# Norm roots by Newton steps on DVE, and transposes between the halves of the output projection, in a two-layer decoder trunk

## The chip, the cores and the metric

The kernel runs on one core of one Trainium2 chip. The core has a matrix engine (PE, with its weight loads PEld), a vector engine (DVE), an activation engine (ACT), a general engine (POOL) and a queue engine (SP) that here only issues DMAs. Each engine takes its instructions strictly in order. The metric is the device time of one execution in microseconds (us).

## What is computed

Two layers on 512 tokens of width 1024. Every sublayer is x += PostNorm(f(PreNorm(x))), and each norm needs one reciprocal root per token:

```python
def rms_norm(x, g):
    y = x * lax.rsqrt(jnp.mean(x * x, axis=-1, keepdims=True) + RMS_EPS)
    return y * g

def reference(...):
    for layer in range(DEPTH):                       # DEPTH = 2
        h = rms_norm(x, mix_pre_g[layer])
        if layer < N_A:                              # layer 0
            m = pool_mixer(h, pool_w[layer], pool_scale[layer])
        else:                                        # layer 1
            ... # k, v from rms_norm(x, kv_norm_g), rope, shared
            m = swa_sink_attention(q, kk, vv, sinks[j]) @ w_o[j]
        x = x + rms_norm(m, mix_post_g[layer])
        f = conv_glu_ffn(rms_norm(x, ffn_pre_g[layer]), ffn_w_in[layer], ffn_conv_w[layer],
                         ffn_conv_b[layer], ffn_w_out[layer])
        x = x + rms_norm(f, ffn_post_g[layer])
    return x
```

conv_glu_ffn is an up-projection to 2 x 2816 channels, a causal convolution of width 3, GeGLU, and a down-projection.

## The kernel before, in words

The 512 tokens are four row blocks of 128 (b = 0 to 3), one token to a partition, so a norm's root is one value per partition: a tile of 128x1. A factor of a product is split into a high and a low part (`wh`/`wl` for weights, `xTh`/`xTl` for activations, `gh`/`gl` for the FFN's hidden values), and a product is three matmuls (`mm3`, lines 306 to 308). The high part is a copy on ACT, the low part a subtraction on DVE, or on POOL in `low` (line 398, through line 193).

**Order.** Line 1147 opens `tc.manual_schedule(engines=ORDERED)`, and ORDERED (line 1131) names PE, ACT, DVE and POOL: on these four the program's order is the order of execution, and only the semaphores between them are added.

**A root.** `rstd_of` (line 243) squares both halves of a row on ACT, each with its sum into a column of `ss` (line 247). After the first half POOL adds epsilon (`add_eps`, 254); after the second, `rstd_end` adds the two sums (257) and raises them to -0.5 (258), both on POOL. There are 32 roots: four blocks times mix_norm, post_norm and pre_norm in layer 0, the FFN's post norm in both layers (`root` in pass2), `pre_a` before the attention, and post_norm and pre_norm after it.

**The stages that hold roots.** I call them A to D.

- A, the mixer of layer 0 (lines 402 to 441). `mix_norm` scales x; `mix_pool` and `mix_map` are matmuls; `post_norm` (264) multiplies by the gain straight from PSUM (272) and adds to x (274); `pre_norm` (286) makes the next input (291); `transpose_in` (294) turns it on PE (299) and splits it (302 on ACT, 303 on DVE). `low` splits the first two units of FFN weights in between, eight quarters in all, on ACT (189) and POOL (193). `start0` then runs the up-projection `up` of the units j = 0 and 1 for blocks 0 and 1, with the transposes of blocks 2 and 3 in between.
- B, the end of the down-projection of layer 0, `pass2` (612). Two block products, X[2] and X[3], are summed over p = 0 to 10. Blocks 2 and 3 are ready early: after p = 0 their sums are added (652), squared (671), rooted, multiplied by the gain (676) and added to x (685). `soon(k)` splits the weights (226, 227) and hidden values (636, 637) that later p need: soon(6) those of p = 6 and 7, soon(7) of 8 and 9, soon(8) of 10. `pre_a` and `pre_b` (278, 282) norm x for the attention, and `to_attention` (770) transposes it. The last three p run for blocks 0 and 2 first (i = 0), then for 1 and 3; blocks 0 and 1 are finished after that, while PE runs the k and v projections (`kp`, `vp`) of blocks 2 and 3.
- C, the output projection after the attention (1043 to 1054) and `start1` (1056): per block `o_proj`, `post_norm`, `low`, `pre_norm`, `low`, with the transposes of blocks 0 and 1 in the turns of blocks 2 and 3; then `up` as in A.
- D, the same as B in layer 1, without attention behind it: the end of the kernel.

SP loads weights through two buffers `raw`; a new load is issued when the split of an older unit is done.

Of the kernel before, what the change touches and what calls it, by code (L numbers as in the profile page):

```python
# [8 lines left out]
F32 = mybir.dt.float32  # L9
F32R = mybir.dt.float32r  # L10
I32 = mybir.dt.int32
AF = mybir.ActivationFunctionType
ALU = mybir.AluOpType
PSUM = bass.MemoryType.PSUM

P = 128
S = 512
D = 1024
# [8 lines left out]
EPS = 1e-6  # L27
# [43 lines left out]
def build(nc, tc, ctx, a, out):  # L71
# [3 lines left out]
    pc = ctx.enter_context(tc.tile_pool(name="pc", bufs=1))  # L75
# [18 lines left out]
    xT = new_xT("f0")  # L94
# [19 lines left out]
        o = ch * 4 + k  # L114
        return convs[l][:, o : o + 1]

    mhalf = pc.tile([P, 1], F32, tag="mhalf", name="mhalf")
    nc.gpsimd.memset(mhalf, -0.5)


    raws, slots, homes = {}, {}, {}
# [118 lines left out]
        return t  # L240


    def rstd_of(src, junk, name):

        ss = pc.tile([P, 4], F32, tag="ss", name=f"ss_{name}", bufs=6)
        for h in range(2):
            nc.scalar.activation(junk[h], src[h], AF.Square, scale=1.0 / math.sqrt(D),
                                 accum_out=ss[:, h : h + 1])
            if h == 0:
                add_eps(ss, 0)  # L250
        return rstd_end(ss)

    def add_eps(ss, h):
        nc.gpsimd.tensor_scalar(ss[:, h : h + 1], ss[:, h : h + 1], EPS, None, ALU.add)  # L254

    def rstd_end(ss):
        nc.gpsimd.tensor_tensor(ss[:, 2:3], ss[:, 0:1], ss[:, 1:2], ALU.add)
        nc.gpsimd.tensor_tensor(ss[:, 3:4], ss[:, 2:3], mhalf, ALU.pow)
        return ss[:, 3:4]

    def halves(t):
        return [t[:, h * 512 : (h + 1) * 512] for h in range(2)]
# [72 lines left out]
    xns, xnf = {}, {}  # L335
# [276 lines left out]
    def pass2(l, p2, G2, X, post_row):  # L612


        Z12 = pc.tile([P, D], F32, tag="bc", name=f"Z12_{l}", bufs=2)
        Z11 = pc.tile([P, D], F32, tag="t4", name=f"Z11_{l}", bufs=3)
        Z2 = pc.tile([P, 4 * D], F32, tag="xTh", name=f"Z2_{l}")
        gx = pc.tile([P, 4 * D], F32R, tag="xTl", name=f"gx_{l}")
        Z = {"11": halves(Z11), "12": halves(Z12), "21": halves(Z2[:, 0:D]), "22": halves(Z2[:, D : 2 * D])}
        gains = halves(post_row)  # L620
        G = {}

        def split2(n, m):
            k = min(4 if n == 2 else 2, NP - (4 if n == 2 else 2) * m)
            if n == 2 and m < 2:

                h, lo = (gx[:, (2 * m + c) * 1024 : (2 * m + c + 1) * 1024] for c in range(2))
            else:
                h, lo = (p2.tile([P, 1024], F32R, tag="g", name=f"{c}{n}_{l}_{m}", bufs=8) for c in ("gh", "gl"))
            if n == 2:  # L630
                g = G2[:, 4 * m : 4 * m + k, 2, :]
                o = [t[:, : k * 256].rearrange("p (k t) -> p k t", t=256) for t in (h, lo)]
            else:
                g = G2[:, 2 * m : 2 * m + k, 0:2, :].rearrange("p k q t -> p k (q t)")
                o = [t[:, : k * 512].rearrange("p (k t) -> p k t", t=512) for t in (h, lo)]
            nc.scalar.copy(o[0], g)
            nc.vector.tensor_tensor(o[1], g, o[0].bitcast(F32), ALU.subtract)  # L637
            G[n, m] = (h, lo)

        homes[U_D2[l] + 1] = homes[U_D3[l] + 2] = homes[U_D3[l] + 5] = (p2, "x")  # L640
        for t in ("whx", "wlx"):
            p2.tile([P, 2048], F32R, tag=t, name=f"first_{t}{l}")
        todo = [(2, 0), (2, 1), (2, 2), *((3, m) for m in range(6))]

        def soon(k):
            if k < len(todo):
                n, m = todo[k]
                split((U_D2 if n == 2 else U_D3)[l] + m)
                split2(n, m)

        def add(z, i, q):
            nc.vector.tensor_tensor(Z[z][i], Z[z][i], X[q][i], ALU.add)

        soon(0)
        for i in range(2):
            nc.scalar.copy(Z["11"][i], X[1][i])
            nc.vector.tensor_tensor(Z["21"][i], Z["11"][i], X[6][i], ALU.add)
        soon(1)
        for i in range(2):
            nc.vector.tensor_tensor(Z["12"][i], Z["21"][i], X[5][i], ALU.add)  # L660
        for q in (4, 2, 3):
            X[q] = [bank(f"dn{l}_{q}_{i}") for i in range(2)]
        ss, rs = {}, {}

        def square(z, i, q):

            b, h = i + (2 if z[0] == "2" else 0), int(z[1]) - 1
            first = b not in ss
            if first:
                ss[b] = pc.tile([P, 4], F32, tag="ss", name=f"ss_p_f{l}{b}", bufs=6)  # L670
            nc.scalar.activation(X[q][i], Z[z][i], AF.Square, scale=1.0 / math.sqrt(D), accum_out=ss[b][:, h : h + 1])  # L671
            if first:
                add_eps(ss[b], h)

        def gain(z, i):
            nc.vector.tensor_tensor(Z[z][i], Z[z][i], gains[int(z[1]) - 1], ALU.mult)

        def root(b):
            rs[b] = rstd_end(ss[b])

        def update(b):
            r = rs[b]
            for h in range(2):
                xs = halves(x[b])[h]
                nc.vector.scalar_tensor_tensor(xs, Z[f"{b // 2 + 1}{h + 1}"][b % 2], r, xs, ALU.mult, ALU.add)
                if l == 1:
                    nc.sync.dma_start(out[b][:, h * 512 : (h + 1) * 512], xs)

        def then(f, b):
            if l == 0:  # L690
                f(b)


        for m in range(3):
            for p in range(4 * m, min(4 * m + 4, NP)):
                product(U_D2[l] + m, (p % 4) * 512, G[2, m], (p % 4) * 256, X[4], (0, 1), p == 0, p == NP - 1)
            soon(m + 2)
            if m < 2:
                nc.vector.tensor_tensor(Z["22"][m], Z["12"][m], X[7][m], ALU.add)
                add("21", m, 7)  # L700
                square("22", m, 7)
            else:
                for i in range(2):
                    gain("22", i)
        of = {3: (512, 256), 2: (0, 0)}

        def make(q, p, is_):
            w, go = of[q]
            o = p % 2
            product(U_D3[l] + p // 2, o * 1024 + w, G[3, p // 2], o * 512 + go, X[q], is_, p == 0, p == NP - 1)  # L710

        NT = 3
        for p in range(NP - NT):
            for q in of:
                make(q, p, (0, 1))
            if p == 0:
                for i in range(2):
                    add("21", i, 4)
                    square("21", i, 4)
                    root(2 + i)  # L720
                soon(5)
                for i in range(2):
                    gain("21", i)
                for i in range(2):
                    update(2 + i)
                soon(6)
            if p == 1:
                then(pre_a, 2)
                then(pre_a, 3)
                soon(7)  # L730
                then(pre_b, 2)
                then(pre_b, 3)
            if p == 5:
                then(to_attention, 2)
                soon(8)
                then(split, U_K)
            if p == 6:
                then(to_attention, 3)

        for i in range(2):  # L740
            for q in of:
                for p in range(NP - NT, NP):
                    make(q, p, (i,))
        then(split, U_V)
        add("12", 0, 3)
        square("12", 0, 3)
        add("11", 0, 2)
        square("11", 0, 2)
        root(0)
        gain("12", 0)  # L750
        gain("11", 0)
        add("12", 1, 3)
        square("12", 1, 3)
        update(0)
        then(pre_a, 0)
        add("11", 1, 2)
        square("11", 1, 2)
        root(1)
        gain("12", 1)
        gain("11", 1)  # L760
        then(pre_b, 0)
        update(1)
        then(pre_a, 1)
        then(pre_b, 1)

# [14 lines left out]
    with tc.tile_pool(name="att", bufs=1, reuse_waits="tile") as pa:  # L780
# [4 lines left out]
        nsink = pa.tile([P, NH], F32, tag="nsink", name="nsink")  # L785
        nc.gpsimd.tensor_scalar(nsink, sink, -1.0, None, ALU.mult)
        tab = pa.tile([P, 1], F32, tag="tab", name="tab")
# [146 lines left out]
        to_attention(1)  # L934
        k_T(3, kst[3])
        split(U_Q)
        nc.scalar.activation(tab, mhalf, AF.Exp)
        kst[0] = k_block(0)
        v_block(0)
        split(U_Q + 1)  # L940
# [4 lines left out]
        acc, xnf = {}, {}  # L945
# [33 lines left out]
        os = {}  # L979
# [62 lines left out]
        xT = new_xT("f1")  # L1042
# [2 lines left out]
        u0, u1 = U_IN[1], U_IN[1] + 1  # L1045
        for b in range(NB):
            u = (u0, u1)[b // 2]
            o_proj(1, b, os[1, b])
            post_norm(b, acc[b], post_row, "m1", pa)
            low(u, b % 2 * 2)  # L1050
            if b > 1:
                transpose_in(b - 2, xnf[b - 2], xT, "f1")
            xnf[b] = pre_norm(b, pre_row, "f1")
            low(u, b % 2 * 2 + 1)

# [94 lines left out]
```

## Time and profile before

| what | value |
|---|---|
| median of 3 runs | 946.09 us (945.75 to 950.86) |
| profiled execution | 945.61 us, of which the span from first to last instruction is 943.5 us |
| busy time over the span | PE 911.8, PEld 781.1, DVE 654.3, ACT 469.5, POOL 337.9 us |
| mean granted TensorE clock | 0.988 of full speed |
| instructions on DVE, POOL | 940, 389 |

The profile is of one execution. Starts are in us from the span's first instruction. A line of a timeline is: start, duration, engine, line of the kernel, operation, output tile <- input tiles, shapes, count, and in brackets the idle time of that engine just before it and what ended it. A line of a group has, after the bar, the total busy time, the mean duration of one in ns, and the idle time before them. Where a timeline merges several instructions (x2, x4), the duration runs from the first start to the last end.

### The profile page before, as it was taken

The page shows a single profiled execution, that of the slowest core. Times are in us where ns is not written, and L with a number is a line of the kernel's source. Part 1 is how long each engine was busy: PE and PEld are TensorE (multiplying, and loading weights), DVE is VectorE, ACT ScalarE, POOL GpSimd, SP SyncE. Part 2 cuts the span into 40 slices and gives each one's busy share as a digit, 9 for nine tenths or more (in the row PEclk, how much of TensorE's full clock was granted, in tenths as well). Part 3 has the DMA queues.
Part 4 walks back from the last instruction along what each step waited for, and adds up shares of the span by engine and source line. Part 5 has one row for each costly group of instructions (what it writes and reads, how often), then busy time and mean ns, then how long its engine had stood idle before and what let it go on. Part 6 is the DMA issues. An engine that isn't in the chain of part 4 may idle for free.

```text
span 943.5 us, 12767 instructions
## 1 busy us (share of the span) xinstructions
PE 911.8 (97%) x4702; PEld 781.1 (83%) x4702; DVE 654.3 (69%) x940; ACT 469.5 (50%) x823; POOL 337.9 (36%) x389
## 2 busy tenths in 40 slices
PE   9999999999999999899999996999999999999996
PEld 8888888888888877799899885988888888888784
DVE  5878888765567788545999747466555565677886
ACT  5645444533345566454788634433333433455562
POOL 3725444433341002325566226144444433410001
PEclk9999999999999999899999997999999999999998
DMA  8356899855555664740112214444555555456652
GB/s 304 123 192 222 324 332 319 296 198 189 190 177 149 217 211 147 278 162 19 45 46 91 90 45 149 142 179 179 187 206 198 197 204 191 160 164 196 222 186 87
DMA packets 43024, 170.10 MB, mean 180 GB/s; under 512 B 5073, under 2 KB 6609, under 8 KB 34898
## 3 DMA queue, kind: packets, MB, share of 16 engines
q1 hardware_dynamic: 41810, 160.90, 48.7%
q10 hardware_dynamic: 1152, 8.39, 2.3%
q8 instruction: 37, 0.61, 0.3%
q14 instruction: 25, 0.20, 0.1%
HBM read 135.72 MB, written 33.55 MB: 179 GB/s over the span
## 4 chain that ended last, share of the span: by engine, by line
PE 76%; DVE 11%; DMA 3%; issue 3%; ACT 3%; POOL 3%; SPq 0%; POOLq 0%; DVEq 0%; ACTq 0%
PE u L307 17%; PE u L308 17%; PE u L306 17%; PE dn L306 4%; PE dn L307 4%; PE dn L308 4%; DVE xn_f L291 2%; DVE wl L227 2%; DVE P L895 1%; DMA raw<-in_ws_dram 1%; DVE x L274 1%; DMA raw<-t 1%; PE op L306 1%; PE op L307 1%; PE op L308 1%
## 5 line engine op out<-in xcount | busy, mean ns | idle before, releaser
L306 PE MATMUL u<-xTh_f,wh 128*128 128x512 f32 (+1 forms) x768 | 286.7, 373 | 4.5 <-ACT xTh_f L302 4.5
L307 PE MATMUL u<-xTl_f,wh 128*128 128x512 f32 (+1 forms) x768 | 286.2, 373 | 4.3 <-DVE xTl_f L303 4.3
L308 PE MATMUL u<-xTh_f,wl 128*128 128x512 f32 (+1 forms) x768 | 286.0, 372 | 0.0
L227 DVE TENSOR_TENSOR wl<-raw,wh 128x1024 fp32r<-128x1024 f32 (+1 forms) x158 | 204.6, 1335 | 14.2 <-ACT wh L226 13.9
L306 PEld LDWEIGHTS u<-xTh_f,wh 128*128 128x128 f32 x768 | 145.6, 190 | 30.1 <-ACT xTh_f L302 5.0
L307 PEld LDWEIGHTS u<-xTl_f,wh 128*128 128x128 f32 x768 | 145.5, 189 | 29.4 <-DVE xTl_f L303 4.8
L524 DVE SCALAR_TENSOR_TENSOR t<-u,conv,t 128x511 f32<-128x511 f32 x88 | 65.8, 748 | 148.0 <-ACT t L523 148.0
L308 PEld LDWEIGHTS u<-xTh_f,wl 128*128 128x128 f32 x768 | 145.5, 189 | 24.9
L226 ACT CAST wh<-raw 128x1024 fp32r<-128x1024 f32 (+1 forms) x158 | 156.8, 1041 | 12.7 <-DMA raw<-t 6.9
L523 ACT ACTIVATE t<-u,conv 128x512 f32<-128x512 f32 x88 | 68.2, 777 | 137.9 <-PE u L308 100.8
L544 POOL TENSOR_TENSOR G<-G,G 128x256 f32<-128x256 f32 x22 | 33.3, 1515 | 278.1 <-DVE G L539 278.1
L307 PE MATMUL dn<-wl,gh 128*128 128x512 f32 x276 | 108.1, 392 | 1.4 <-DVE wl L227 1.4
L308 PE MATMUL dn<-wh,gl 128*128 128x512 f32 x276 | 108.0, 391 | 1.2 <-DVE gl L637 1.2
L306 PE MATMUL dn<-wh,gh 128*128 128x512 f32 x276 | 108.1, 392 | 0.0
L532 ACT ACTIVATE t<-t 128x512 f32<-128x512 f32 x44 | 27.8, 632 | 104.6 <-DVE t L525 104.6
L525 DVE SCALAR_TENSOR_TENSOR t<-u,conv,t 128x510 f32<-128x510 f32 x88 | 65.9, 749 | 3.1
L307 PEld LDWEIGHTS dn<-wl,gh 128*128 128x128 f32 x276 | 52.1, 189 | 13.0 <-DVE wl L227 2.3
L254 POOL TENSOR_SCALAR ss_p_f<-ss_p_f 128x1 f32<-128x1 f32 x8 | 2.8, 354 | 166.6 <-ACT dn L671 166.6
L308 PEld LDWEIGHTS dn<-wh,gl 128*128 128x128 f32 x276 | 52.1, 189 | 12.4 <-DVE gl L637 1.6
L306 PEld LDWEIGHTS dn<-wh,gh 128*128 128x128 f32 x276 | 52.2, 189 | 10.8
L565 ACT CAST gh<-G 128x1024 fp32r<-128x1024 f32 x22 | 23.1, 1052 | 55.3 <-DVE G L563 40.8
L566 DVE TENSOR_TENSOR gl<-G,gh 128x1024 fp32r<-128x1024 f32 x22 | 28.0, 1274 | 26.6 <-ACT gh L565 21.1
(194 smaller groups left out, 1555.0 us busy)
## 6 DMA issues: line engine op xcount, KB each, us to landing
raw<-in_ws_dram SPq DMA_DIRECT2D x51, 1024.0 KB, 4.9
q<-in_ws_dram SPq DMA_DIRECT2D x44, 512.0 KB, 5.8
raw<-t SPq DMA_DIRECT2D x24, 768.0 KB, 5.5
t<-q SPq DMA_DIRECT2D x44, 256.0 KB, 2.9
t<-q SPq DMA_DIRECT2D x22, 512.0 KB, 2.7
raw<-in_ws_dram SPq DMA_DIRECT2D x22, 512.0 KB, 4.4
raw<-in_ws_dram SPq DMA_DIRECT2D x22, 256.0 KB, 3.9
r<-in_ws_dram SPq DMA_DIRECT2D x8, 512.0 KB, 7.0
```

Of the source, the lines that this page charges most:

```text
L226: nc.scalar.copy(hi[:, s], r[:, s])
L227: nc.vector.tensor_tensor(lo[:, s], r[:, s], hi[:, s].bitcast(F32), ALU.subtract)
L306: nc.tensor.matmul(acc, ah, bh, start=first, stop=False)
L307: nc.tensor.matmul(acc, ah, bl, start=False, stop=False)
L308: nc.tensor.matmul(acc, al, bh, start=False, stop=last)
L523: nc.scalar.activation(t, u, AF.Identity, bias=conv_col(l, ch, 3), scale=conv_col(l, ch, 2))
L524: nc.vector.scalar_tensor_tensor(t[:, 1:], u[:, : S - 1], conv_col(l, ch, 1), t[:, 1:], ALU.mult, ALU.add)
L525: nc.vector.scalar_tensor_tensor(t[:, 2:], u[:, : S - 2], conv_col(l, ch, 0), t[:, 2:], ALU.mult, ALU.add)
L532: nc.scalar.activation(tg, tg, AF.Gelu_apprx_tanh)
L544: nc.gpsimd.tensor_tensor(s1, s1, G2[:, p, 2, :], ALU.add)
L565: nc.scalar.copy(h, G1[:, o : o + 1024])
L566: nc.vector.tensor_tensor(lo, G1[:, o : o + 1024], h.bitcast(F32), ALU.subtract)
```

## The change

The sum of a norm's two halves, epsilon, and the root all move from POOL to DVE. A starting value is made from the bits of the number by a shift and a multiply-add, and three Newton steps of two instructions follow: nine instructions of 128x1 for each root. The squares carry a factor 0.5 in their scale for this. The tile `mhalf` goes, and with it its use as the input of a table load (937).

The order changes too. In `pass2` the gains of blocks 2 and 3 come each before their root, and soon(6) before the updates; pre_a, soon(7) and pre_b move from p = 1 to p = 2; `to_attention(2)` moves from behind p = 5 to behind p = 7, and `to_attention(3)` from behind p = 6 to behind the first half of the tail. For blocks 0 and 1 the roots come behind the gains, and pre_a(0) behind the root of block 1. After the attention, the transposes of block 0 stand behind `o_proj` of block 2, ahead of its post_norm, and those of block 1 between the two halves of `o_proj` of block 3.

```diff
-    mhalf = pc.tile([P, 1], F32, tag="mhalf", name="mhalf")
-    nc.gpsimd.memset(mhalf, -0.5)
...
+    def square(junk, src, ss, h):
+        nc.scalar.activation(junk, src, AF.Square, scale=math.sqrt(0.5 / D), accum_out=ss[:, h : h + 1])
+
+    def new_ss(name):
+        return pc.tile([P, 5], F32, tag="ss", name=f"ss_{name}", bufs=7)
+
+    def rstd_end(ss):
+        v, y, n = ss[:, 2:3], ss[:, 3:4], ss[:, 4:5]
+        iv, iy = v.bitcast(I32), y.bitcast(I32)
+        nc.vector.tensor_scalar(v, ss[:, 0:1], ss[:, 1:2], 0.5 * EPS, ALU.add, ALU.add)
+        nc.vector.tensor_scalar(iy, iv, 1, None, ALU.logical_shift_right)
+        nc.vector.tensor_scalar(iy, iy, -1, 0x5F3759DF - 0x400000 - 2 ** 31, ALU.mult, ALU.add)
+        for _ in range(3):
+            nc.vector.scalar_tensor_tensor(n, y, v, y, ALU.mult, ALU.mult)
+            nc.vector.scalar_tensor_tensor(y, n, 1.5, y, ALU.subtract, ALU.mult)
+        return y
+
     def rstd_of(src, junk, name):
-        ss = pc.tile([P, 4], F32, tag="ss", name=f"ss_{name}", bufs=6)
+        ss = new_ss(name)
         for h in range(2):
-            nc.scalar.activation(junk[h], src[h], AF.Square, scale=1.0 / math.sqrt(D),
-                                 accum_out=ss[:, h : h + 1])
-            if h == 0:
-                add_eps(ss, 0)
+            square(junk[h], src[h], ss, h)
         return rstd_end(ss)
-
-    def add_eps(ss, h):
-        nc.gpsimd.tensor_scalar(ss[:, h : h + 1], ss[:, h : h + 1], EPS, None, ALU.add)
-
-    def rstd_end(ss):
-        nc.gpsimd.tensor_tensor(ss[:, 2:3], ss[:, 0:1], ss[:, 1:2], ALU.add)
-        nc.gpsimd.tensor_tensor(ss[:, 3:4], ss[:, 2:3], mhalf, ALU.pow)
-        return ss[:, 3:4]
...
             if p == 0:
                 for i in range(2):
                     add("21", i, 4)
-                    square("21", i, 4)
-                    root(2 + i)
+                    square_of("21", i, 4)
                 soon(5)
                 for i in range(2):
                     gain("21", i)
+                    root(2 + i)
+                soon(6)
                 for i in range(2):
                     update(2 + i)
-                soon(6)
-            if p == 1:
+            if p == 2:
                 then(pre_a, 2)
                 then(pre_a, 3)
                 soon(7)
                 then(pre_b, 2)
                 then(pre_b, 3)
             if p == 5:
-                then(to_attention, 2)
                 soon(8)
                 then(split, U_K)
-            if p == 6:
-                then(to_attention, 3)
+            if p == 7:
+                then(to_attention, 2)
 
         for i in range(2):
             for q in of:
                 for p in range(NP - NT, NP):
                     make(q, p, (i,))
+                if i == 0 and q == 3:
+                    then(to_attention, 3)
         then(split, U_V)
         add("12", 0, 3)
-        square("12", 0, 3)
+        square_of("12", 0, 3)
         add("11", 0, 2)
-        square("11", 0, 2)
-        root(0)
+        square_of("11", 0, 2)
         gain("12", 0)
         gain("11", 0)
+        root(0)
         add("12", 1, 3)
-        square("12", 1, 3)
+        square_of("12", 1, 3)
         update(0)
-        then(pre_a, 0)
         add("11", 1, 2)
-        square("11", 1, 2)
-        root(1)
+        square_of("11", 1, 2)
         gain("12", 1)
         gain("11", 1)
+        root(1)
+        then(pre_a, 0)
+        update(1)
         then(pre_b, 0)
-        update(1)
         then(pre_a, 1)
         then(pre_b, 1)
...
-        nc.scalar.activation(tab, mhalf, AF.Exp)
+        nc.scalar.activation(tab, nsink[:, 0:1], AF.Exp)
...
         for b in range(NB):
             u = (u0, u1)[b // 2]
-            o_proj(1, b, os[1, b])
+            o_proj(1, b, os[1, b], (0,))
+            if b == 3:
+                transpose_in(1, xnf[1], xT, "f1")
+            o_proj(1, b, os[1, b], (1,))
+            if b == 2:
+                transpose_in(0, xnf[0], xT, "f1")
             post_norm(b, acc[b], post_row, "m1", pa)
             low(u, b % 2 * 2)
-            if b > 1:
-                transpose_in(b - 2, xnf[b - 2], xT, "f1")
             xnf[b] = pre_norm(b, pre_row, "f1")
             low(u, b % 2 * 2 + 1)
```

More of the change, by code (lines that the diff above doesn't have):

```diff
@@ L663, in pass2, with square_of @@
         ss, rs = {}, {}
[L665 to L673, printed above, removed]
+        def square_of(z, i, q):
+            b = i + (2 if z[0] == "2" else 0)
+            if b not in ss:
+                ss[b] = new_ss(f"p_f{l}{b}")
+            square(X[q][i], Z[z][i], ss[b], int(z[1]) - 1)
         def gain(z, i):
@@ L700, in pass2 @@
                 add("21", m, 7)
-                square("22", m, 7)
+                square_of("22", m, 7)
             else:
```

## The prediction

> **What bounds the kernel now.** I read the page's busy times and chain first, then PE's table of waits, then PE, DVE and POOL around each wait.
>
> ```profile
> PE 911.8 (97%) x4702; PEld 781.1 (83%) x4702; DVE 654.3 (69%) x940; ACT 469.5 (50%) x823; POOL 337.9 (36%) x389
> ...
> PE 76%; DVE 11%; DMA 3%; issue 3%; ACT 3%; POOL 3%; SPq 0%; POOLq 0%; DVEq 0%; ACTq 0%
> ```
>
> ```profile
> PE tr_a L299 <- ACT xn_a L284: 6.1, 1, 6.1
> PE u L306 <- ACT xTh_f L302: 4.5, 2, 4.3
> PE u L307 <- DVE xTl_f L303: 4.3, 2, 3.9
> ```
>
> PE is full, and the two long layers of products carry three quarters of the chain. It waits in few places, and these are the norms: 6.1 us in stage B, 4.3 and 3.9 us in stage C. In A and at the end of D the norms are the chain as well. So the 32 roots are cheap in total and dear where they stand: what a root costs is the time from ACT's second sum to DVE's next step in those chains. Elsewhere PE is dense, and a delay before a dense stretch comes out whole at the end.
>
> **A root on POOL.** Timeline of block 0 in stage A:
>
> ```profile
> 19.82 2.24 DVE L274 SCALAR_TENSOR_TENSOR x<-pt_m,ss_p_m,x 128x512 f32<-128x512 f32 x2
> ...
> 22.63 0.19 ACT L247 ACTIVATION_READ_ACCUMULATOR xn_f<-x 128x1 f32 x1
> ...
> 22.96 0.19 POOL L257 TENSOR_TENSOR ss_n_f<-ss_n_f 128x1 f32<-128x1 f32 x1 [0.50 <-ACT xn_f L247]
> ...
> 23.24 0.57 POOL L258 TENSOR_TENSOR ss_n_f<-ss_n_f,mhalf 128x1 f32<-128x1 f32 x1
> ...
> 23.84 2.41 DVE L291 SCALAR_TENSOR_TENSOR xn_f<-x,ss_n_f,fpre 128x512 f32<-128x512 f32 x2 [1.78 <-POOL ss_n_f L258]
> ```
>
> x is done at 22.06, its squares 0.8 us later at 22.82, and DVE goes on at 23.84: a root costs 1.02 us. In a post_norm it costs less, as the gains (272) run on DVE beside it.
>
> **A root on DVE.** Nine instructions of one column, each needing the one before. The trace has none of 128x1, so I bound one from rows of the same kinds (groups by form, then two dependent steps of a timeline):
>
> ```profile
> L876 DVE DVE_READ_ACCUMULATOR2_ANT stat<- 128x1 f32 x64 | 5.0, 78 | 0.0
> ...
> L892 DVE RECIPROCAL stat<-stat 128x4 f32<-128x4 f32 x16 | 2.8, 178 | 7.0 <-POOL stat L888 7.0
> ...
> L469 DVE SCALAR_TENSOR_TENSOR rope_tmp<-rope_tmp 128x128 f32<-128x128 f32 x4 | 1.2, 291 | 0.1
> ...
> L460 DVE TENSOR_SCALAR rope_tmp<-freq 128x32 f32<-128x32 f32 x4 | 0.7, 235 | 0.0
> ```
>
> ```profile
> 55.91 0.23 DVE L461 TENSOR_SCALAR rope_tmp<-rope_tmp 128x128 f32<-128x128 f32 x1
> 56.17 0.23 DVE L462 TENSOR_SCALAR rope_tmp<-rope_tmp 128x128 f32<-128x128 f32 x1
> ```
>
> Below 0.078 us (a read-out that computes nothing) and above 0.291 us (128 columns) one can't lie. Nearest are the 4 columns, 0.178 us, and the 32 with a per-partition scalar, 0.235 us. I take 0.16 us for the five with constants, 0.21 us for the four with a column as scalar, and 0.03 us between dependent steps (start to start 0.26 us for 0.23 us): 9 x 0.03 + 5 x 0.16 + 4 x 0.21 = **R = 1.9 us**, from 0.7 (9 x 0.078) to 2.9 us (9 x 0.32). That is 0.9 us more than POOL's, and it stands in DVE's order, where gains and subtractions wait behind it.
>
> [...]
>
> **What POOL and DVE take from each other.**
>
> ```profile
> L291 DVE SCALAR_TENSOR_TENSOR xn_f<-x,ss_n_f,fpre 128x512 f32<-128x512 f32 x16 | 21.4, 1377 | 10.0 <-POOL ss_n_f L258 10.0
> ...
> L274 DVE SCALAR_TENSOR_TENSOR x<-pt_m,ss_p_m,x 128x512 f32<-128x512 f32 x16 | 16.2, 1053 | 0.3 <-POOL ss_p_m L258 0.3
> ...
> L685 DVE SCALAR_TENSOR_TENSOR x<-Z,ss_p_f,x 128x512 f32<-128x512 f32 x16 | 11.1, 746 | 1.7 <-POOL ss_p_f L258 1.4
> ```
>
> The same shape takes 0.746 us at 685, where POOL is idle, and 1.377 and 1.053 us where `low` runs: 16 x 0.631 + 16 x 0.307 = 15 us of blocking in A and C. `low` still runs after the change, so I keep 7 us of it in A's chain and 6 in C's; it may hit the small steps instead, or fall into waits.
>
> **Stage A.** Groups of DVE, and the end of the last norm:
>
> ```profile
> 12.13 3.22 DVE L360 SCALAR_TENSOR_TENSOR wp<-raw,cst,scale_row 128x256 f32<-128x256 f32 x8 [1.16 <-DMA raw<-in_ws_dram]
> ```
>
> ```profile
> 46.89 3.44 DVE L291 SCALAR_TENSOR_TENSOR xn_f<-x,ss_n_f,fpre 128x512 f32<-128x512 f32 x2 [1.79 <-POOL ss_n_f L258]
> ```
>
> ```profile
> 50.48 0.63 PE L299 MATMUL tr_f<-cst,xn_f 128*128 128x128 f32 x4 [1.04 <-DVE xn_f L291]
> ```
>
> DVE's unit prices are in the next fence (369.19 to 375.32): a pair of gains 1.2, a pair of updates 1.35, a weight unit 3.4; a pair of subtractions (303) counts 1.2 like the gains, xm I estimate at 0.8 from them. The end of 360 at 15.35 stays; then three roots, two xm, gains and update: 15.35 + 5.7 + 1.6 + 1.2 + 1.35 = 25.2 (22.06 before). From there to the last xn: 7 roots 13.3, 3 gains 3.6, 7 updates or xn 9.5, 2 subtractions 2.4, 4 waits for squares 3.2: 57.2, with 7 of blocking 64.2. Before: 50.33, and PE waited for it. **+14 us**, from +7 (no blocking).
>
> **Stage B.**
>
> ```profile
> 369.19 1.29 DVE L676 TENSOR_TENSOR Z<-Z,fpost 128x512 f32<-128x512 f32 x2
> 370.40 2.73 DVE L685 SCALAR_TENSOR_TENSOR x<-Z,ss_p_f,x 128x512 f32<-128x512 f32 x4
> 373.05 2.35 DVE L227 TENSOR_TENSOR wl<-raw,wh 128x1024 fp32r<-128x1024 f32 x2
> 375.32 1.21 DVE L637 TENSOR_TENSOR gl<-G,gh 128x1024 fp32r<-128x1024 f32 x1
> ```
>
> ```profile
> 372.71 7.29 POOL L257 TENSOR_TENSOR ss_n_a<-ss_n_a 128x1 f32<-128x1 f32 x1 [0.16 <-ACT xn_a L247]
> ```
>
> ```profile
> 381.44 1.97 PE L299 MATMUL tr_a<-cst,xn_a 128*128 128x128 f32 x8 [6.15 <-ACT xn_a L284]
> ```
>
> ```profile
> 372.00:384.00 12.00, 5.85 (x25) 4.84 (x24) 8.21 (x9) 8.05 (x15) 9.36 (x6) 0.79 0.40 146
> ```
>
> ```profile
> 413.00 0.36 PE L306 MATMUL kp<-wh,xTh_a 128*128 128x256 f32 x1
> ```
>
> Here the change has its reason. An addition of one column, 0.19 us elsewhere, took 7.29 us on POOL while DVE ran one two-input subtraction after the other; PE stood 6.15 us behind it, and the granted clock fell to 0.79. That goes. What is late next is DVE: gains and two roots from 369.2 end at 374.2, soon(6) at 377.6, so p = 6, due at 375.3, waits 2 us. Updates (2.7) and two more roots end at 384.0, soon(7) at 387.4; ACT's casts and pre_b let `to_attention(2)` start near 385, 2 us after p = 7, and p = 8 waits another 1.5 for soon(7). No idle is long, so I count the clock full, and PE reaches the k projection some 2 us early. Blocks 0 and 1 then take that back: four roots, 7.6, with updates, gains, adds and squares hold DVE until about 410, the rotations of `kp` stand behind them in DVE's order, and the products of block 0 that started at 413.0 start near 415. **+2 us**, from -2 to +4. The moved transposes issue 16 matmuls, four copies and four subtractions, no DMA; the loads of U_K and U_V on ACT's queue keep their order; U_K's comes some 5 us later, behind soon(8), and `kp` needs it a dozen products later still.
>
> **Stage C.**
>
> ```profile
> 556.95 0.19 ACT L247 ACTIVATION_READ_ACCUMULATOR pt_m<-op 128x1 f32 x1
> ```
>
> ```profile
> 583.31 0.58 PE u L307
> ```
>
> Before, `up` began in full at 583.3 (the second row is from the chain in order of time). After: from 557.1, six roots 11.4, three gains 3.6, six updates or xn 8.1, two subtractions 2.4, three waits 2.4: 585.0, with 6 of blocking 591. The transposes' new places take block 1's subtraction ahead of the last post_norm, which the sum holds; but PE now waits at `tr_f` for xn(1) with a half of `o_proj` behind it, and as only the last post_norm squares that half, behind all of this sum, I cost that at nothing. **+8 us**, from +2.
>
> **Stage D.**
>
> ```profile
> 914.97 1.29 DVE L676 TENSOR_TENSOR Z<-Z,fpost 128x512 f32<-128x512 f32 x2
> ...
> 938.89 1.42 DVE L685 SCALAR_TENSOR_TENSOR x<-Z,ss_p_f,x 128x512 f32<-128x512 f32 x2 [0.73 <-POOL ss_p_f L258]
> ```
>
> Gains, two roots and soon(6) end at 914.97 + 1.2 + 3.8 + 3.4 = 923.4, where before it was about 922.3 (it waited for a DMA there): +1, and I estimate another 1 for soon(7) and soon(8). In the tail two roots, 3.8, replace waits of 0.73 and less: +3. **+5 us**, from +3.
>
> **Sum:** 14 + 2 + 8 + 5 = +29 on the profiled execution's 945.6 (median 946.1): **975 us**. SP's queue slides with A and C, since the load of ffn_post_g waits for the last gain; the dense products behind cover it, else it would add the few us of a load.
>
> **Rivals.**
> 1. *POOL wins every gap between the small steps.* Six of the nine read two tiles in SBUF, and the blocked rows above say such steps wait for POOL. With all of POOL's work in the two stages in the way, the 15 us of blocking double: near 986 us. Against it: some of `low` falls into waits. [...] Chance 0.14.
> 2. *A small step is cheap* (not slower). Some 10 + 4 + 6 + 4 roots lie on the path, so 29 us vanish when R falls by 1.2 us, at R = 0.7, the lower bound: 946 us, no change. For it only the 0.078 us row; against it the 0.178 and 0.26 us rows. [...] Chance 0.06.
> 3. *PE was waiting for POOL alone.* If DVE keeps ahead of PE in B and C, B's 6.15 us with its clock and C's 4.3 + 3.9 go, A and D cost their lower bounds (10): 945.6 - 6.15 - 2.5 (12 us at 0.21 under full clock) - 8.2 + 10, near 939. Against it: C's last releaser is DVE already. Chance 0.08.
>
> That the change isn't executed as written is excluded, as the four engines keep program order.
>
> **How the numbers follow.** Forecast 0.72. The range takes the lower bounds of A to D (7 - 2 + 2 + 3 = +10, 956) and, above, the first rival with B at its upper end: **956 to 988**. 0.5% (5 us) is about what a measurement can tell: faster 0.08 (rival 3, a little of 2), within 0.04, slower 0.88.
>
> **What would show it.** Nine steps of 0.16 to 0.24 us per root on DVE; DVE near 710 us, POOL without 128x1 work; PE idle for several us before `tr_f` in A; no 7 us instruction on POOL in B; `up` of layer 1 starting some 25 us later in the span (A, B and C together). I am wrong if the roots' steps overlap, or if A's last xn comes within 5 us of 50.3.

## The result and the profile after

The changed kernel takes **978.31 us** (median of 4 runs, 976.44 to 979.97), the one before 945.92 us beside it (944.30 to 950.86): a ratio of 1.033, 95% interval 1.029 to 1.038, slower. The profiled execution took 979.87 us, 978.1 of them in the span. The forecast was 975 us, 956 to 988.

The page of the changed kernel: busy times, then the chain that ended last, by engine.

```profile
PE 927.6 (95%) x4702; PEld 789.4 (81%) x4702; DVE 707.0 (72%) x1228; ACT 469.3 (48%) x823; POOL 293.5 (30%) x292
...
PE 71%; DVE 18%; ACT 3%; issue 3%; DMA 3%; POOL 1%; SPq 0%; DVEq 0%; ACTq 0%; POOLq 0%
```

DVE has 288 more instructions (nine for each of 32 roots) and 53 us more work; its share of the chain rose from 11 to 18%, and PE's fell from 76 to 71%. PE issues the same 4702 products. PE's table of waits says where it now stands:

```profile
PE tr_f L305 <- DVE xn_f L297: 16.7, 8, 5.5
PE u L313 <- DVE xTl_f L309: 5.6, 3, 4.5
PE dn L314 <- DVE gl L643: 5.0, 4, 1.8
PE u L312 <- ACT xTh_f L308: 2.4, 2, 2.2
PE pd L381 <- DVE xm L347: 2.4, 1, 2.4
```

The wait of 6.1 us for `xn_a` (stage B before) is gone from the head of the table. In its place PE waits 16.7 us for the norms' outputs `xn_f` in A and C (2.6 us before), where every transpose needs two more roots of DVE's chain.

One root in the changed kernel: DVE's timeline in A, block 0's post norm, and POOL's row at the same time.

```profile
25.84 0.21 DVE L252 TENSOR_SCALAR ss_p_m<-ss_p_m 128x1 f32<-128x1 f32 x1 [2.12 <-ACT pt_m L243]
26.09 0.15 DVE L253 TENSOR_SCALAR ss_p_m<-ss_p_m 128x1 int32<-128x1 int32 x1
26.27 0.15 DVE L254 TENSOR_SCALAR ss_p_m<-ss_p_m 128x1 int32<-128x1 int32 x1
26.46 1.21 DVE L256 SCALAR_TENSOR_TENSOR ss_p_m<-ss_p_m 128x1 f32<-128x1 f32 x1
27.71 0.16 DVE L257 SCALAR_TENSOR_TENSOR ss_p_m<-ss_p_m 128x1 f32<-128x1 f32 x1
...
28.68 1.29 DVE L278 TENSOR_TENSOR pt_m<-my,mpost 128x512 f32<-128x512 f32 x2
29.89 1.41 DVE L280 SCALAR_TENSOR_TENSOR x<-pt_m,ss_p_m,x 128x512 f32<-128x512 f32 x2
```

```profile
26.39 1.27 POOL L191 TENSOR_TENSOR wl<-raw,wh 128x512 fp32r<-128x512 f32 x1 [25.96 <-ACT wh L187]
```

The steps come one after the other. A step of one column that reads two tiles took 1.21 us beside POOL's subtraction of 1.27 us, which had started 0.07 us earlier. DVE's groups by form (group | us in all, mean ns) show how often that happens:

```profile
L297 DVE SCALAR_TENSOR_TENSOR xn_f<-x,ss_n_f,fpre 128x512 f32<-128x512 f32 x16 | 16.3, 1058 | 0.4
L256 DVE SCALAR_TENSOR_TENSOR ss_n_f<-ss_n_f 128x1 f32<-128x1 f32 x24 | 12.6, 527 | 0.9
L256 DVE SCALAR_TENSOR_TENSOR ss_p_m<-ss_p_m 128x1 f32<-128x1 f32 x24 | 7.7, 319 | 0.9
L257 DVE SCALAR_TENSOR_TENSOR ss_n_f<-ss_n_f 128x1 f32<-128x1 f32 x24 | 6.9, 287 | 0.8
L256 DVE SCALAR_TENSOR_TENSOR ss_p_f<-ss_p_f 128x1 f32<-128x1 f32 x24 | 5.3, 219 | 0.9
L257 DVE SCALAR_TENSOR_TENSOR ss_p_f<-ss_p_f 128x1 f32<-128x1 f32 x24 | 3.8, 159 | 0.8
L252 DVE TENSOR_SCALAR ss_p_f<-ss_p_f 128x1 f32<-128x1 f32 x8 | 1.7, 208 | 0.0
L254 DVE TENSOR_SCALAR ss_p_f<-ss_p_f 128x1 int32<-128x1 int32 x8 | 1.2, 153 | 0.3
```

Undisturbed (`ss_p_f`, stages B and D, where POOL stands idle beside the roots) a root is 208 + 2 x 154 + 3 x (219 + 159) ns and nine gaps of 34 ns: 1.96 us. In A and C the means of 527, 287 and 319 ns add 24 x (0.308 + 0.128 + 0.100) = 12.9 us of blocking to the roots, while the 16 `xn` fell from 1377 to 1058 ns. Most of it stands beside `low` (12 steps, 11.4 us); at the end of A it is POOL's sums of down-projection weights (lines 559 to 562) that DVE's steps meet (two steps, 1.4 us).

**By stage.** The starts of the products that end each stage, read from PE's timelines, give the lengths below in us. A runs to the first product of `up` in layer 0 after PE's last wait, B from the first product of the down-projection to the k projection of the second pair of blocks (413.0 before), C from the first product of `op` to `up` of layer 1 after PE's last wait, D from the first product of the second down-projection to the end. PE at the end of A, in B and at the end of C of the changed kernel:

```profile
70.02 1.29 PE L305 MATMUL tr_f<-cst,xn_f 128*128 128x128 f32 x8 [3.36 <-DVE xn_f L297]
71.07 0.36 PE L312 MATMUL u<-xTh_f,wh 128*128 128x256 f32 x1
...
398.11 0.50 PE L314 MATMUL dn<-wh,gl 128*128 128x512 f32 x1 [1.77 <-DVE gl L643]
...
613.01 0.58 PE L313 MATMUL u<-xTl_f,wh 128*128 128x256 f32 x1 [4.51 <-DVE xTl_f L309]
```

| kernel | A | B | C | D | the rest | span |
|---|---|---|---|---|---|---|
| before | 50.9 | 130.0 | 66.3 | 115.0 | 581.3 | 943.5 |
| changed | 71.1 | 130.4 | 74.8 | 119.4 | 582.3 | 978.1 |
| difference | +20.2 | +0.4 | +8.5 | +4.4 | +1.0 | +34.6 |
| forecast | +14 | +2 | +8 | +5 | | +29 |

### The profile page after: what moved, and what is told of

It reads as the page before. It is cut to its first block, busy times and chain, and to the rows that moved or that the text cites. A ratio compares the mean times of both kernels' runs of the same rounds, so it can differ in the third digit from the quotient of the medians.

```text
span 978.1 us, 12894 instructions
## 1 busy us (share of the span) xinstructions
PE 927.6 (95%) x4702; PEld 789.4 (81%) x4702; DVE 707.0 (72%) x1228; ACT 469.3 (48%) x823; POOL 293.5 (30%) x292
## 4 chain that ended last, share of the span: by engine, by line
PE 71%; DVE 18%; ACT 3%; issue 3%; DMA 3%; POOL 1%; SPq 0%; DVEq 0%; ACTq 0%; POOLq 0%
PE u L313 16%; PE u L314 16%; PE u L312 16%; PE dn L314 3%; PE dn L312 3%; PE dn L313 3%; DVE wl L225 3%; DVE xn_f L297 1%; DVE P L899 1%; DMA raw<-in_ws_dram 1%; DVE gl L643 1%; DVE ss_n_f L256 1%; ACT wh L224 1%; DMA raw<-t 1%; PE op L312 1%
## 5 line engine op out<-in xcount | busy, mean ns | idle before, releaser
L313 PEld LDWEIGHTS u<-xTl_f,wh 128*128 128x128 f32 x768 | 146.3, 190 | 31.3 <-DVE xTl_f L309 6.4
L191 POOL TENSOR_TENSOR wl<-raw,wh 128x512 fp32r<-128x512 f32 x21 | 28.4, 1354 | 97.6 <-ACT wh L187 97.6
```

What stands on the lines that cost most here:

```text
L191: (low or nc.vector).tensor_tensor(lo, r, hi.bitcast(F32), ALU.subtract)
L313: nc.tensor.matmul(acc, ah, bl, start=False, stop=False)
```

## The experiments

Theory: the cost is the nine-step chain itself, in DVE's order, on 22 to 24 of the 32 roots. Rivals: the new order costs; POOL's blocking costs; the granted clock costs.

### Each half of the change alone

`e1_order_only` has the changed order with before's `add_eps` and `rstd_end` on POOL; `e2_roots_only` has before's order with the Newton steps.

```diff
 # e1_order_only, against the changed kernel (add_eps as before)
-        nc.vector.tensor_scalar(v, ss[:, 0:1], ss[:, 1:2], 0.5 * EPS, ALU.add, ALU.add)
...
+        nc.gpsimd.tensor_tensor(ss[:, 2:3], ss[:, 0:1], ss[:, 1:2], ALU.add)
+        nc.gpsimd.tensor_tensor(ss[:, 3:4], ss[:, 2:3], mhalf, ALU.pow)
```

> The changed order of issue with the roots back on POOL. My theory (the roots' length in the norm chains costs all of it, the order costs nothing): A returns to before's, its last xn at 50.3 us; B is 2 to 5 us faster than before, since root 2 and root 3 are no longer ahead of soon(5) and DVE is free sooner; C within 4 us of before; the whole 936 to 948 us. Rival (the order itself costs, because PE waits at tr_f behind a half of the output projection and the K transposes of block 2 and 3 come later): 950 us or more, with the loss in C and B.

> Before's order of issue with the nine-step roots on DVE. My theory: A as in the changed kernel, its first product of the layer about 20 us later than before; B loses what the new order avoided (two roots ahead of soon(5) and soon(6): 4 to 8 us more than the changed kernel), C within 4 us of the changed kernel; the whole 976 to 990 us. Rival (the order costs and the roots don't in B to D): below 970 us.

Measured: order alone 943.77 us, ratio 0.996 (0.994 to 0.998); roots alone 990.9 us, ratio 1.047 (1.043 to 1.051), 0.9 us above the range expected.

| kernel | A | B | C | D | the rest | span |
|---|---|---|---|---|---|---|
| order only | 54.5 | 125.4 | 64.0 | 116.1 | 582.3 | 942.3 |
| roots only | 71.1 | 137.1 | 78.0 | 122.3 | 583.5 | 991.9 |

Over all the order costs nothing: it gains 4.6 us in B and 2.3 in C, and loses 1.1 in D. Its last `xn` in A isn't back at 50.3 us, as expected, but at 54.0, though A has before's order: in that execution the granted clock was half from about 12.6 to 19.4 us, of which more below. With the roots on DVE the order is worth more, 6.6 us in B, 3.2 in C, 2.8 in D; by the program, it takes roots out of the way of `soon(5)` and `soon(6)`. So the two halves of the change have opposite signs, and against the order alone the roots cost 16.6 + 5.0 + 10.8 + 3.3 = 35.7 us.

The 7.29 us addition on POOL, the reason for the change in B, is gone by the order alone. POOL's timeline in `e1_order_only`:

```profile
369.36 0.19 POOL L251 TENSOR_TENSOR ss_p_f<-ss_p_f 128x1 f32<-128x1 f32 x1 [6.94 <-ACT dn L245]
369.63 0.56 POOL L252 TENSOR_TENSOR ss_p_f<-ss_p_f,mhalf 128x1 f32<-128x1 f32 x1
...
381.13 0.47 POOL L251 TENSOR_TENSOR ss_n_a<-ss_n_a 128x1 f32<-128x1 f32 x1 [0.17 <-ACT xn_a L245]
```

The addition for `ss_n_a` now meets no long stretch of DVE's subtractions and takes 0.47 us.

### How long the chain is

```diff
 # e5_two_steps
-        for _ in range(3):
+        for _ in range(2):
             nc.vector.scalar_tensor_tensor(n, y, v, y, ALU.mult, ALU.mult)
```

> The changed kernel with two Newton steps per root instead of three (the root is less exact): 0.219 + 0.159 + 2 x 0.034 = 0.45 us less for each of 32 roots. My theory (the length of the dependent chain on DVE is the cost, some 24 of the roots stand on a path): about 11 us less, 964 to 971 us, of it 5 or more before the first layer's products and 4 in stage C. Rival (what costs is POOL's blocking, and it only shifts to the next instruction): 974 us or more.

Measured: 968.18 us, 10.1 us less, as the theory has it. A is 67.8 us (3.3 less, where 5 were expected), B 127.6 (2.8 less), C 72.2 (2.6 less, where 4 were expected), D 117.9 (1.5 less). The blocking didn't go with the steps: the means of 527, 287 and 319 ns rose to 618, 351 and 428 over 16 steps each in place of 24, 16 x (0.399 + 0.192 + 0.209) = 12.8 us, as much as before this edit. So each of the 32 roots is 0.45 us shorter, and by an estimate 10.1 / 0.45 = 22 of them stand on a path.

### Whether POOL's blocking is the cost

```diff
 # e3_one_input
-            nc.vector.scalar_tensor_tensor(n, y, v, y, ALU.mult, ALU.mult)
-            nc.vector.scalar_tensor_tensor(y, n, 1.5, y, ALU.subtract, ALU.mult)
+            nc.vector.tensor_scalar(n, y, y, v, ALU.mult, ALU.mult)
+            nc.vector.tensor_scalar(y, n, 1.5, y, ALU.subtract, ALU.mult)
 # e6_low_one, in piece()
-            (low or nc.vector).tensor_tensor(lo, r, hi.bitcast(F32), ALU.subtract)
+            if low is None:
+                nc.vector.tensor_tensor(lo, r, hi.bitcast(F32), ALU.subtract)
+            else:
+                low.tensor_scalar(lo, r, 2.0 ** -13, None, ALU.mult)
```

> The changed kernel with its six Newton instructions per root written with one tile input and a column as scalar in place of two tile inputs; the arithmetic is the same up to rounding. If the small steps lose time to POOL because they read two tiles: their means fall from 319 and 527 ns to about 220 ns in A and C, 6 to 13 us less in all, 966 to 973 us. Rival (the blocking only moves to the updates and subtractions of two inputs that stand behind them, which then take their 1053 and 1377 ns again): within 4 us of 978. Second rival (POOL blocks one-input steps as well): the means stay.

Measured: 976.25 us, ratio 1.032 (1.029 to 1.035), only 2 us less. DVE's groups by form:

```profile
L256 DVE TENSOR_SCALAR ss_n_f<-ss_n_f 128x1 f32<-128x1 f32 x24 | 6.5, 273 | 0.9
L256 DVE TENSOR_SCALAR ss_p_f<-ss_p_f 128x1 f32<-128x1 f32 x24 | 6.6, 273 | 0.9
L257 DVE TENSOR_SCALAR ss_n_f<-ss_n_f 128x1 f32<-128x1 f32 x24 | 5.1, 214 | 0.8
L297 DVE SCALAR_TENSOR_TENSOR xn_f<-x,ss_n_f,fpre 128x512 f32<-128x512 f32 x16 | 14.3, 932 | 0.3
```

The blocking of the small steps is gone: beside POOL (`ss_n_f`) and without POOL (`ss_p_f`) they have the same mean. It did not move to the instructions behind them (`xn` 932 ns, less than the 1058 before the edit). But a step became 54 to 55 ns dearer (273 for 219, 214 for 159), 0.33 us a root; by an estimate, 22 roots on a path take back 7 us. The price of the other form I had put at nothing. The stages show both sides: A is 64.4 us (6.7 less than in the changed kernel) and C 70.7 (4.1 less), where POOL's subtractions stand, but B is 136.0 (5.6 more) and D 121.5 (2.0 more), where there is nothing to unblock. Of A's 6.7 some 4 may be the granted clock, which in this execution stayed full until 29.7 us (below). So the run doesn't measure the blocking by itself.

> The changed kernel, where POOL's 16 subtractions in A and C (low half = weight minus rounded weight) are replaced by a product of the weight with a constant, of the same size but with one input (those low halves are then not the reference's). If POOL's two-input instructions hold up DVE's small steps and subtractions: the means of the steps are back at 219 and 159 ns, x_n at 746 ns, from block 0's update to the last xn 31 to 33 us in place of 39.2, C 4 to 6 us shorter, the whole 964 to 969 us. Rival (any POOL instruction on SBUF does it): within 3 us of 978.

Measured: 964.33 us, ratio 1.019 (1.016 to 1.022), the 14 us expected, but for a mixed reason. Without the high part as an input, POOL no longer waits for ACT's copy, and in A its first seven products ran in one stretch that ended at 31.0 us, ahead of the norms of blocks 1 to 3; POOL's timeline:

```profile
19.83 11.19 POOL L194 TENSOR_SCALAR wl<-raw 128x512 fp32r<-128x512 f32 x7
```

Besides, the edit reaches the quarters that are split during the attention, and the mean granted clock of the profiled execution was 0.986 in place of the changed kernel's 0.976; a full clock early in A alone is worth some 4 us (below). The means didn't fall all the way (320 ns for 219 in `ss_n_f`, `xn` 820), and from block 0's update to the last `xn` A took 34.0 us, where 31 to 33 were expected. So the run can't say whether an instruction of one input blocks less; it says that with most of POOL's blocking out of the way, the changed kernel is still some 20 us above the order alone.

### The place of POOL's subtractions, with either root

The 2 x 2 that tells length from blocking: roots on POOL or DVE, the 16 subtractions of `low` on POOL or DVE.

```diff
     def low(i, q):
-        piece(i, q, nc.gpsimd)
+        piece(i, q)
```

> The changed order with the roots on POOL, and POOL's 16 subtractions in A and C given to DVE at the same places of the order. My theory (DVE waits there for squares and root anyway, and POOL no longer holds up DVE's subtractions): x_n back to about 746 ns, A and C 2 to 4 us shorter each than with the changed order alone, 936 to 940 us. Rival (16 x 0.68 us come on top of a full DVE): 946 to 952 us.

> The changed kernel, roots on DVE, with POOL's 16 subtractions of A and C given to DVE as well; against the kernel at 933.7 us it differs in the place of the roots alone, and POOL has nothing two-input left in A's and C's norms. If the change costs 34 us mostly because the chain of nine steps is long and stands in DVE's order: still 27 to 36 us above 933.7, 961 to 970 us. Rival (mostly because POOL's subtractions hold up the small steps, 14 us by the run with one-input instructions): 14 us or more of the gap gone, below 955 us.

| ratio to before (median) | `low` on POOL | `low` on DVE |
|---|---|---|
| roots on POOL, changed order | 0.996 (943.77 us) | 0.986, 0.984 to 0.989 (933.66 us) |
| roots on DVE, changed order | 1.033 (978.31 us) | 1.024, 1.021 to 1.027 (969.49 us) |

`e8_low_dve` came 2 us below the range of its theory. The roots on DVE cost 3.7% with POOL's subtractions beside them, and 3.8% without: 35 us either way. So the loss doesn't need `low` on POOL; the chain in DVE's order is enough. Both kinds of roots gain about alike: with them on POOL, 10 us go when `low` moves to DVE, with them on DVE 9. The theory's bound (961 to 970 us) held. DVE's groups show how far the blocking is gone (the first two rows with the roots on DVE, the third with them on POOL):

```profile
L297 DVE SCALAR_TENSOR_TENSOR xn_f<-x,ss_n_f,fpre 128x512 f32<-128x512 f32 x16 | 11.3, 749 | 0.4
L256 DVE SCALAR_TENSOR_TENSOR ss_p_m<-ss_p_m 128x1 f32<-128x1 f32 x24 | 7.5, 313 | 0.9
...
L297 DVE SCALAR_TENSOR_TENSOR xn_f<-x,ss_n_f,fpre 128x512 f32<-128x512 f32 x16 | 13.4, 878 | 7.8 <-POOL ss_n_f L252 6.6 <-ACT xTh_f L308 1.2
```

What is left, 24 x 0.094 = 2.2 us and 16 x 0.132 = 2.1, stands beside POOL's weight sums at the end of A. By stage the roots cost 16.6 + 4.5 + 8.6 + 3.6 us without `low` on POOL, where it was 16.6 + 5.0 + 10.8 + 3.3 with it, so some 2 us of C may be blocking. (Early in A, both executions of the pair with `low` on POOL had a half clock, for 10.2 and 6.8 us. Neither of the other pair shows one there: `e13_roots_low_dve` had 1.00 from 8 to 28 us, and for `e8_low_dve` the pace of its products says so, below.) That none of the 35 us is blocking isn't shown: the move also puts 16 subtractions of 0.68 us into DVE's order, and these may weigh more where DVE is the chain.

Why a root costs more than the 0.94 us by which its chain is longer is seen in the same stretch of both, from block 0's `xn` to block 1's. DVE with the roots on POOL (`e8_low_dve`):

```profile
22.86 1.41 DVE L297 SCALAR_TENSOR_TENSOR xn_f<-x,ss_n_f,fpre 128x512 f32<-128x512 f32 x2 [1.18 <-POOL ss_n_f L252]
24.19 0.68 DVE L193 TENSOR_TENSOR wl<-raw,wh 128x512 fp32r<-128x512 f32 x1
24.79 1.28 DVE L278 TENSOR_TENSOR pt_m<-my,mpost 128x512 f32<-128x512 f32 x2
25.99 1.40 DVE L280 SCALAR_TENSOR_TENSOR x<-pt_m,ss_p_m,x 128x512 f32<-128x512 f32 x2
27.31 0.68 DVE L193 TENSOR_TENSOR wl<-raw,wh 128x512 fp32r<-128x512 f32 x1
27.92 1.28 DVE L309 TENSOR_TENSOR xTl_f<-tr_f,xTh_f 128x512 fp32r<-128x512 f32 x2
29.17 0.75 DVE L297 SCALAR_TENSOR_TENSOR xn_f<-x,ss_n_f,fpre 128x512 f32<-128x512 f32 x1
```

And with them on DVE (`e13_roots_low_dve`):

```profile
28.00 1.42 DVE L297 SCALAR_TENSOR_TENSOR xn_f<-x,ss_n_f,fpre 128x512 f32<-128x512 f32 x2
...
29.94 0.21 DVE L252 TENSOR_SCALAR ss_p_m<-ss_p_m 128x1 f32<-128x1 f32 x1
...
31.78 1.28 DVE L278 TENSOR_TENSOR pt_m<-my,mpost 128x512 f32<-128x512 f32 x2
32.98 1.41 DVE L280 SCALAR_TENSOR_TENSOR x<-pt_m,ss_p_m,x 128x512 f32<-128x512 f32 x2
34.30 0.69 DVE L191 TENSOR_TENSOR wl<-raw,wh 128x512 fp32r<-128x512 f32 x1
34.91 1.28 DVE L309 TENSOR_TENSOR xTl_f<-tr_f,xTh_f 128x512 fp32r<-128x512 f32 x2
36.10 0.21 DVE L252 TENSOR_SCALAR ss_n_f<-ss_n_f 128x1 f32<-128x1 f32 x1
...
38.07 1.41 DVE L297 SCALAR_TENSOR_TENSOR xn_f<-x,ss_n_f,fpre 128x512 f32<-128x512 f32 x2
```

The first takes 29.17 - 22.86 = 6.31 us, the second 38.07 - 28.00 = 10.07: 3.76 us more for two roots, 1.88 each. On POOL neither of the two shows, since gains, `low` and the split of the transposes run on DVE meanwhile. DVE does wait for POOL's roots elsewhere in A: 1.18 us ahead of block 0's `xn`, 0.73 and 1.19 ahead of block 2's and 3's. On DVE each root takes its whole length out of the same order. Over all, 35 us on 22 roots are by this estimate 1.6 us each, between the 0.94 and the 1.96.

> The kernel before with nothing changed but POOL's 16 subtractions of A and C given to DVE. Theory: the gain of 10 us is that of the subtractions alone and the changed order adds its 2 us: 934 to 938 us. Rival (the order and the place of the subtractions need each other): 940 us or more.

Measured: 938.55 us, ratio 0.991 (0.987 to 0.994), half a microsecond above the range of the theory. The move of `low` alone gains 7 to 9 us, and the changed order adds 4 to 5 to it, not the 2 expected: with the changed order and the roots left on POOL it is 933.66 us, **faster than both kernels**, by 1.4% of the kernel before (1.1 to 1.6). A of that kernel takes 47.2 us, B 125.7, C 61.0, D 116.0.

### The granted clock in A

PE in the changed kernel stood idle from 10.46 to 12.81 us, for the second block's `xm` with its root; then the clock fell. Windows (start:end length, busy us of PE, PEld, DVE, ACT, POOL; then granted clock, DMA share and GB/s) of the changed kernel:

```profile
10.00:12.00 2.00, 0.46 (x2) 0.02 (x1) 1.45 (x8) 1.23 (x4) 0.00 (x0) 1.00 0.98 395
...
14.00:24.00 10.00, 10.00 (x36) 9.01 (x36) 7.27 (x28) 3.95 (x12) 0.00 (x0) 0.50 0.77 304
```

PE is busy from 14 to 24 us and gets 36 products done. Block 0's post norm waits for them: its root starts at 25.84 after DVE stood still for 2.12 us (the first fence of DVE rows above).

```diff
     mix_weights()
+    keep_busy(5)
     mix_norm(2)
```

> The changed kernel with five more 128x128 products that nobody reads, issued on PE in A ahead of the third mixer norm, where PE stood 2.36 us idle at 10.5 us. If the first half of A was late because the granted clock fell to a half from 13.4 to 23.6 us after that idle time: the half clock there is gone, block 0's update is done 3 to 5 us earlier (31.3 us in the changed kernel), the whole near 973 to 975 us. Rival (DVE's chain of roots sets block 0's update whatever PE's clock): within 1.5 us of 978.

The same windows with the five products (ten instructions in the trace):

```profile
10.00:12.00 2.00, 1.96 (x14) 1.64 (x12) 1.31 (x8) 1.37 (x4) 0.00 (x0) 1.00 0.98 395
...
14.00:24.00 10.00, 10.00 (x62) 9.17 (x62) 9.13 (x37) 5.24 (x15) 1.53 (x1) 1.00 0.76 303
```

The clock stays full, 62 products in place of 36, and block 0's update is done at 26.73 us, 4.56 earlier. `up` starts 4.0 us earlier, at 67.05. The whole is 976.31 us, ratio 1.032 (1.029 to 1.035), 2 us less, between the two expectations, and its interval overlaps the changed kernel's. Of the 4.0 us some 1.4 are gone again by the first product of the down-projection: the clock is half from 64 to 70 us, and products of `up` run in it. Nor does every such wait lead to it: `e3_one_input` waits 1.40 and 2.15 us at the same place, and its clock there is full (1.00 from 8 to 28 us). The four executions of `e6_low_one` fall into two pairs, 962.4 and 962.5 us at a mean granted clock of 0.986, 966.1 and 966.4 at 0.981; that this is the same stretch isn't shown. So of A's 20.2 us about 4 belong to this clock in the profiled execution; that the median carries 2 of them fits, but isn't shown. Nor is it the roots' alone: the order alone, with POOL's roots, had a half clock after a wait of 1.48 us.

> The kernel before this one in this call, with five more 128x128 products that nobody reads ahead of the third mixer norm. If the granted clock falls to a half after PE's wait for the second mixer norm and A pays for it: no half clock ahead of block 0's update, another 2 to 3.6 us less. Rival (DVE and POOL set A whatever the clock): within 1.5 us of the one without them.

Measured: 933.69 us, the same as without them. There was nothing to win: in the profile of `e8_low_dve` PE waits 0.5 and 0.8 us for `xm`, and its first 32 products for `my` take 7.00 us from 13.90 on, as in the kernel before (7.15 us at a granted clock of 1.00), where the changed kernel's take 9.71.

## Why the prediction was right, step by step

- **The root's length.** Forecast 1.9 us, measured 1.96 undisturbed; 0.16 us for the steps with constants measured 0.154 and 0.159, 0.21 for those with a column 0.208 and 0.219. The second rival (R = 0.7 us) falls.
- **What it replaces.** "0.9 us more than POOL's" was too little as a price of the move: POOL's root lay beside DVE's work, so on a path the move costs about 1.6 us. The sums were made of whole chains, in which R counts in full, so the 0.9 enters none of them. The 24 roots that the second rival counts on the path are 22 by the run with two steps.
- **Stage A, the term that was mis-sized.** Forecast +14, measured +20.2. The end of block 0's update was put at 25.2 us and came at 31.3, because PE had the half clock there; at full clock it came at 26.7 (`e4_warm`), and A was +16.2. The forecast looked at PE's waits for each norm, not at the half clock that followed the early wait of 2.36 us. From that update to the last `xn` the forecast had 39 us; the changed kernel took 39.2 (31.29 to 70.54). That it fits so closely is luck: by DVE's timeline the blocked rows there add up to 8.7 us in place of 7, and DVE waited for squares only twice, 0.79 and 0.80 us, in place of four times 0.8.
- **Stage B.** Forecast +2 by a gain of 2 us at the k projection and a loss of 4 behind it. Measured: `kp` starts 18.0 us later than before where A had left 20.2, so 2.2 gained, and the second pair 20.6 later, +0.4, so 2.6 lost. The wait foreseen at p = 6 (2 us) was 1.77 us for `gl`; a second of 1.16 us followed, where 1.5 were foreseen.
- **Stage C.** Forecast +8, measured +8.5. The table of waits has the mechanism: 5.5 us at a transpose for `xn`, then 4.5 us for the last `xTl`. Half of `o_proj` stands behind that transpose, and the order alone, which has it too, gains 2.3 us in C, so no cost of it shows.
- **Stage D.** Forecast +5, measured +4.4. From the first product to the last it took 109.1 us in place of 107.3 (+1.8, where 2 were forecast), and what stands behind the last product 10.3 in place of 7.7 (+2.6, where 3 were).
- **The rivals.** The first, POOL winning each gap, is seen in single rows (1.21 us for a step), and the blocking grew to 12.9 us on small steps and 5 on `xn` (16 x 0.31), 18 against 15 before, but it didn't double. By the 2 x 2, the loss is there with most of the blocking gone. POOL's 7.29 us row spans six whole instructions of DVE (373.05 to 379.93 us in the kernel before), so it is no wait for a single one. The rival's 986 us doesn't follow from its words: 30 us of blocking in place of the 13 in the sum would give 992. The third, PE waiting for POOL alone, falls, since the change made the kernel slower. Its reasoning on B was right, as the order alone, with POOL's roots, gains 4.6 us there, but it needs the roots to stay on POOL.

In all the median came 3.3 us above the forecast. The profiled execution rose by 34.6 us where the sum had 29: A took 6.2 more than its term, and the other terms nearly cancel. `up` of layer 1 started 29.7 us later, where 25 were named as a sign, and A's last `xn` ended 20.2 us behind the 50.3, where within 5 would have spoken against the forecast.

## What to carry to other kernels

An operation that is moved between engines is priced by what it shows on the path in each place: here a short chain on an idle engine, hidden beside the work of a busy one, cost nothing (two roots on POOL within the 6.31 us from `xn` to `xn`), and the chain in its place on the busy one cost nearly its whole length (1.88 us a root of 1.96). Where a change joins a new order with a new place of work, try each alone; here the order gained 7 us in two stages, and the place lost 35. Where two engines hold each other up, it was worth more here to move the big operation off one of them (7 to 10 us) than to rewrite the small ones that suffer (2 us).

## What the runs showed of the hardware

- A DVE step with a single tile input and columns as scalars wasn't held up by POOL: 273 and 214 ns in every stage (`e3_one_input`), where the form with two tiles went from 219 and 159 to a mean of 527 and 287 ns (the changed kernel).
- A column as a scalar cost 54 to 60 ns: 208 against 154 and 219 against 159 ns in place of a constant, 273 against 219 and 214 against 159 in place of a second tile. With constants a step of one column took 153 to 159 ns.
- Waits of like length (2.36 us in the changed kernel, 2.15 us in `e3_one_input`) were followed by 10.2 us at half the granted clock in one and by a full clock until 29.7 us in the other. No run here shows what decides it.
